# A two-layer diffusion backbone on one core: the first modulation vectors by pieces of columns, sums of squares as products, one tile for two activations

## The chip, the cores and the metric

One core of a Trainium2 chip runs the whole network in one launch. The metric is device time in microseconds (us), the median of several executions. Beside them stands one profiled execution with its own time, from which all durations are taken.

## What is computed

The reference runs two layers over 256 context tokens and 256 latent tokens of width 1024. What matters here is how a layer begins:

```python
m_lat = split(silu(c) @ w_ada[l] + b_ada[l], 9)          # shift, scale, gate for three sub-layers
m_ctx = split(silu(c_ctx) @ w_ada[l] + b_ada[l], 9)
x   = x + 0.5 * gate * swiglu(rmsnorm(x, g) * (1 + scale) + shift)     # FFN, w1 1024 x 5632, w2 2816 x 1024
...                                                                     # mixers, a second FFN
```

So the first FFN of layer 0 needs, before its first product, the root mean square of every token and two of the nine vectors of `w_ada[0]` (shift and scale, 1024 columns each), for both kinds of token.

## The kernel before

Activations are held transposed: `x` is [128 partitions, 8 chunks of features, 512 tokens], context tokens first. Every dense product is float32 in three float32r products: a weight tile [128 x 1024] is loaded as `raw`, cast on ScalarE to `whi` (`split`, L219), and VectorE makes the rest `wlo` (L220); the activations are split the same way into a high and a low half. `three` (L232 to L234) then adds up high x low, high x high and low x high; I call these three products a triple. Each triple that calls `tick()` moves the object `beside` one step on, and generators that were registered with `beside.at(gen, ticks)` run their next part at those ticks: that is how norms, attention stages and loads are put between products. The order on TensorE is the program's own; a scheduler orders the other engines by priority (`tc.high_priority`) and by edges (`tc.issue_after`).

`cold_start` (L413) is the begin of layer 0. `square_sum` (L252) squares a chunk on ScalarE and adds it on VectorE into `ssq`, 16 times; `rstd_cols` and `rstd_rows` (L260, L276) make rows of 1/rms through TensorE. `ada_first` (L158) makes one quarter of shift and scale: 512 columns of `w_ada0` in four DMAs of 512 KB, with packets of 2 KB, each followed by 8 small products of `sc` (the SiLU of c and c_ctx in a 32 wide weight) at L169, then a copy (L174), a transposition (L177) and a few VectorE operations of 4 elements (L182, L184). `norm_part` (L286) makes one chunk of the normed input `h` for one kind of token: `u` on VectorE (L289), the high half on ScalarE (L291), the low half on VectorE (L292). The first halves of scale and shift come before the first triple; the second halves are made by `beside` at the ticks of `COLD`, between the triples of chunks 0 to 3 of the six first weight tiles (two tiles at a time, 24 triples). Then the 24 triples of chunks 4 to 7 follow. All these loads go through one queue, SP's, in the program's order.

Later in the layers, `h` (input of an FFN or of the mixers) and `y` (the merged mixer output) are two tiles with one tag and one buffer, so that the first write of the one waits for the last read of the other. Stages of attention heads run at the ticks listed in `A0`, `A3` and `AT_LAT`.

Of the kernel before, what the change touches and what calls it, by code (L numbers as in the profile page):

```python
# [16 lines left out]
P = 128  # L17
# [23 lines left out]
A0 = (10, 12, 18, 20, 23, 25, 27, 30, 32, 35, 37, 39)  # L41
# [5 lines left out]
              n=(14, 17, 29, 32, 36, 39), n3=(14, 20, 34, 40, 46, 52))  # L47
AT_FULL = dict(d0=A0, d=A1, d3=A2, n=A3, n3=A4)
NORM = (400, 4, 0)
SPREAD = (360, 440, 360, 1)  # L50
EARLY = 2
COLD = ((4, 6, 8, 10, 12, 13), (10, 12, 14, 16, 17, 18))
# [59 lines left out]
def tile_backbone(ctx: ExitStack, tc: tile.TileContext, I, out: bass.AP):  # L112
# [45 lines left out]
    def ada_first(l, mod, part, room):  # L158

        pa = psum()  # L160
        c0 = mod * D + part * 512
        for k2 in range(KC // 2):
            raw = room[:, k2, :]
            nc.sync.dma_start(out=raw.rearrange("p (k c) -> p k c", k=2),
                              in_=I["w_ada0"][k2 * 256:(k2 + 1) * 256, c0:c0 + 512].rearrange("(k p) c -> p k c", k=2))
            for k in range(2):
                kc = 2 * k2 + k
                for j in range(4):
                    mm(pa[32 * j:32 * j + 32, 0:P], sc[:, kc, :], raw[:, k * 512 + j * P:k * 512 + (j + 1) * P],  # L169
                       start=kc == 0, stop=kc == KC - 1)  # L170
            yield
        rows = np_.tile([P, 256], F32, tag="rows", name="rows", bufs=1)[:, 0:P]
        with tc.high_priority(offset=AHEAD):
            nc.scalar.copy(rows, pa[:, 0:P])  # L174
        yield
        pt = psum()
        nc.tensor.transpose(pt[:, 0:P], rows, ident)  # L177
        ks = slice(4 * part, 4 * part + 4)
        v = pt[:, 0:P].rearrange("p (j c) -> p j c", j=4)
        with tc.high_priority(offset=AHEAD):  # L180
            for cls in range(2):
                nc.vector.tensor_tensor(modT[l][:, mod, cls, ks], v[:, :, cls], b_ada[:, l, mod, ks], ALU.add)  # L182
                if mod % 3 == 1:
                    nc.vector.scalar_tensor_tensor(amod[l][:, mod // 3, cls, ks], modT[l][:, mod, cls, ks], 1.0,  # L184
                                                   norm_g[:, l, mod // 3, ks], ALU.add, ALU.mult)
# [30 lines left out]
    def split(hi, lo, src, behind=None):  # L216

        with tc.issue_after(behind) if behind else nullcontext():
            nc.scalar.copy(hi, src)  # L219
        nc.vector.tensor_sub(lo, src, hi.bitcast(F32))  # L220

    def weights(src, n=1024, extra=None, soon=False, room=None, behind=None):
# [3 lines left out]
        with tc.high_priority(offset=AHEAD if soon else WSOON):  # L226
            split(hi[:, :n], lo[:, :n], raw[:, :n], behind)
        return hi, lo
# [21 lines left out]
    ssq = cp.tile([P, T], F32, name="ssq")  # L250

    def square_sum(dt, cs):  # L252
# [4 lines left out]
        nc.scalar.activation(sq, x[:, dt, cs], AF.Square)  # L257
        nc.vector.tensor_tensor(ssq[:, cs], ssq[:, cs], sq, ALU.add)

    def rstd_cols(cs):  # L260
# [6 lines left out]
        with tc.high_priority(offset=AHEAD):  # L267
            nc.vector.tensor_reduce(out=r[:, :n], in_=p1[:, 0:n * P].rearrange("p (t c) -> p t c", t=n),
                                    axis=AX.X, op=ALU.add)
            nc.vector.tensor_scalar(r[:, :n], r[:, :n], 1.0 / D, EPS, ALU.mult, ALU.add)  # L270
            nc.gpsimd.tensor_tensor(r[:, :n], r[:, :n], half[:, :n], ALU.pow)
# [14 lines left out]
    def norm_part(l, which, h, kc, cls, rb):  # L286
# [5 lines left out]
        nc.vector.scalar_tensor_tensor(h[1][:, kc, cs], u, shift, h[0][:, kc, cs].bitcast(F32),  # L292
                                       ALU.add, ALU.subtract)
# [67 lines left out]
    def ada_all(vectors, pool, junk):  # L361
        if not vectors:
            return
        scb = pool.tile([P, 2, 512], F32, name="scb")
# [12 lines left out]
    def ffn(l, i, classes, out_classes_next, before, vectors):  # L377
# [4 lines left out]
        h = split_pair("h") if both else before  # L382
# [30 lines left out]
        def cold_start(n):  # L413

            rooms = glo.before(F32, [P, KC, 1024])
            scale, shift = ([ada_first(l, 3 * which + what, part, rooms[:, 4 * (1 - what):4 * (1 - what) + 4, :])
                             for part in (0, 1)] for what in (1, 0))
            for dt in range(KC):
                for at in SLICES:
                    square_sum(dt, at)  # L420
            rows = [rstd_rows(at) for at in SLICES]
            next(scale[0])
            for r in rows:
                next(r)
            rb = junk.rearrange("p (a t) -> p a t", a=2)
            for cls, r in enumerate(rows):
                next(scale[0])
                nc.scalar.copy(rb[:, cls], next(r)[:, 0:256])
            ws = []

            def load(ks):
                for k in ks:
                    ws.append(w1_unit(k, room=kept(k) if k < 4 else None, soon=k < 2))

            for _ in scale[0]:
                pass
            load(range(EARLY))
            for _ in shift[0]:
                pass
            load(range(EARLY, n))  # L440
            pts = [psum() for _ in range(n)]
            beside.at(scale[1], COLD[0])
            beside.at(shift[1], COLD[1])
            for part, order in enumerate(((0, 2, 4), (4, 0, 2))):
                if part:
                    beside.drain()
                with tc.high_priority(offset=AHEAD):
                    for kc in range(4 * part, 4 * part + 4):
                        for cls in (0, 1):
                            norm_part(l, which, h, kc, cls, rb[:, cls])  # L450
                for k in order:
                    for kc in range(4 * part, 4 * part + 4):
# [4 lines left out]
                    if part:  # L457
                        act(k // 2, pts[k], pts[k + 1])
# [74 lines left out]
        for j in range(FIRST // 2 if cold else 2 if both else 1, NF):  # L533
# [4 lines left out]
            else:  # L538
                ws = [w1_unit(k) for k in (2 * j, 2 * j + 1)]
# [60 lines left out]
    def mixers(l, before):  # L600
# [10 lines left out]
        h = split_pair("h", not full)  # L611
# [566 lines left out]
        for hp2 in range(3):  # L1178
            spread([do(merge, 1, hp2, oT, do(na_qk, hp2 + 1))], na_pair(hp2), 3 * nb, 38, AT["n"])
# [7 lines left out]
        y = split_pair("y", not full)  # L1187
# [15 lines left out]
        def ended(dt, pt):  # L1203
            for cls in (0, 1) if full else (1,):
                residual(l, 1, dt, pt, cls, True)
            if not full:

                with tc.high_priority(offset=AHEAD):
# [176 lines left out]
```

## Time and profile before

| what | value |
|---|---|
| median of 3 executions | 2267.32 us (2265.69 to 2268.48) |
| the profiled execution | 2266.51 us, of which 2264.7 us are the span from the first to the last instruction |
| TensorE (PE) busy | 2234.9 us, 99% of the span |
| VectorE (DVE) busy | 1579.1 us, 70% |
| ScalarE (ACT) busy | 934.4 us, 41% |
| bytes moved | 315.53 MB, 139 GB/s on average |

A slice of the span is read best by its stage: the begin, where nothing is loaded yet, has other limits than the rest, where TensorE has no gap for hundreds of microseconds. PE is the products' own row, PEld the loading of weights beside them, SP the queue of DMAs.

### The profile page before, as it was taken

Reading aid. Unit: us, or ns where it says so; the run is one execution under the profiler, and the core shown is the slowest. Engines: PE = TensorE matmul, PEld = TensorE weight load, DVE = VectorE, ACT = ScalarE, POOL = GpSimd, SP = SyncE. Lnnn points to the kernel's source line nnn. Section 1 sums busy time; section 2 is a strip of 40 time slices with the busy share of each in tenths; the row PEclk is TensorE's granted clock in tenths of the full one; section 3 lists DMA queues with packets and bytes.
Section 4 is the critical chain, followed back from the end, with each engine's and each line's share of the span. In section 5 each row is a group of like instructions: output and inputs, shape, how many; then the busy total and the mean of one; then the engine's idle time right before and its main releaser. Section 6 shows DMA issues by size and latency. Waiting matters only on the chain.

```text
span 2264.7 us, 33530 instructions
## 1 busy us (share of the span) xinstructions
PE 2234.9 (99%) x12799; PEld 1935.7 (85%) x12799; DVE 1579.1 (70%) x3388; ACT 934.4 (41%) x1675; POOL 81.3 (4%) x137
## 2 busy tenths in 40 slices
PE   7999999999999999999999999999999999999998
PEld 4888889888888888888888898888898898899998
DVE  5989843887665664676666579998258885768664
ACT  4323222455654553333222232322234675656443
POOL 0000000001001110000000000000000001200000
PEclk9999999999999999999999999999999999999999
DMA  8556542322223332344544436666333244445564
GB/s 305 184 198 204 192 139 89 112 66 75 75 76 93 91 87 84 99 144 140 159 147 149 141 113 208 208 200 195 101 99 112 67 140 121 135 155 169 188 184 131
DMA packets 94033, 315.53 MB, mean 139 GB/s; under 512 B 12928, under 2 KB 13712, under 8 KB 93872
## 3 DMA queue, kind: packets, MB, share of 16 engines
q1 hardware_dynamic: 89072, 308.07, 42.3%
q0 software_dynamic: 2144, 4.36, 1.4%
q8 instruction: 100, 1.64, 0.3%
q10 hardware_dynamic: 2656, 0.96, 0.2%
q14 instruction: 61, 0.50, 0.1%
HBM read 312.30 MB, written 1.05 MB: 138 GB/s over the span
## 4 chain that ended last, share of the span: by engine, by line
PE 86%; issue 9%; DVE 3%; DMA 1%; ACT 1%; SPq 0%; POOLq 0%; POOL 0%; DVEq 0%; ACTq 0%
PE p L232 25%; PE p L233 24%; PE p L234 24%; PE p L649 2%; PE p L650 2%; PE p L651 2%; PE p L674 1%; PE p L916 1%; PE p L1131 1%; PE p L971 1%; PE p L970 1%; PE p L1041 1%; DMA room<-in_w_ada 1%; PE p L893 1%; DVE wlo L220 1%
## 5 line engine op out<-in xcount | busy, mean ns | idle before, releaser
L219 ACT CAST whi<-raw 128x1024 fp32r<-128x1024 f32 (+1 forms) x430 | 444.7, 1035 | 823.7 <-PE p L233 715.7
L220 DVE TENSOR_TENSOR wlo<-raw,whi 128x1024 fp32r<-128x1024 f32 (+1 forms) x430 | 516.6, 1202 | 268.5 <-ACT whi L219 266.8
L232 PE MATMUL p<-h,whi 128*128 128x512 f32 (+1 forms) x1856 | 695.5, 375 | 0.2 <-DVE h L292 0.2
L234 PE MATMUL p<-h,wlo 128*128 128x512 f32 (+1 forms) x1856 | 681.1, 367 | 0.0
L233 PE MATMUL p<-h,whi 128*128 128x512 f32 (+1 forms) x1856 | 681.1, 367 | 0.0
L232 PEld LDWEIGHTS p<-h,whi 128*128 128x128 f32 x1856 | 348.7, 188 | 58.7 <-issue 2.4
L234 PEld LDWEIGHTS p<-h,wlo 128*128 128x128 f32 x1856 | 348.6, 188 | 58.4
L233 PEld LDWEIGHTS p<-h,whi 128*128 128x128 f32 x1856 | 349.1, 188 | 56.5 <-issue 1.9
L233 PE MATMUL p<-ghi,whi 128*128 128x256 f32 (+1 forms) x836 | 278.0, 333 | 0.0
L234 PE MATMUL p<-ghi,wlo 128*128 128x256 f32 (+1 forms) x836 | 277.8, 332 | 0.0
L197 DVE SCALAR_TENSOR_TENSOR junk<-raw,scb 128x512 f32<-128x512 f32 x256 | 176.2, 688 | 112.7 <-DMA raw<-in_w_adaT 112.2
L232 PE MATMUL p<-glo,whi 128*128 128x256 f32 (+1 forms) x616 | 201.9, 328 | 0.0
L197 DVE SCALAR_TENSOR_TENSOR raw<-raw,scb 128x512 f32<-128x512 f32 x256 | 176.8, 690 | 6.2
L233 PEld LDWEIGHTS p<-ghi,whi 128*128 128x128 f32 x836 | 157.9, 189 | 15.4
L234 PEld LDWEIGHTS p<-ghi,wlo 128*128 128x128 f32 x836 | 157.8, 189 | 15.5
L232 PE MATMUL p<-y,whi 128*128 128x256 f32 (+1 forms) x472 | 136.6, 289 | 0.0
L233 PE MATMUL p<-y,whi 128*128 128x256 f32 (+1 forms) x472 | 136.5, 289 | 0.0
L234 PE MATMUL p<-y,wlo 128*128 128x256 f32 (+1 forms) x472 | 136.2, 289 | 0.0
L232 PEld LDWEIGHTS p<-glo,whi 128*128 128x128 f32 x616 | 116.3, 189 | 10.4
L310 DVE SCALAR_TENSOR_TENSOR x<-p,gmod,x 128x256 f32<-128x256 f32 x80 | 36.5, 480 | 81.8 <-PE p L234 81.7
L232 PEld LDWEIGHTS p<-y,whi 128*128 128x128 f32 x472 | 88.7, 188 | 1.8 <-issue 0.2
L233 PEld LDWEIGHTS p<-y,whi 128*128 128x128 f32 x472 | 88.7, 188 | 1.5
(258 smaller groups left out, 2955.6 us busy)
## 6 DMA issues: line engine op xcount, KB each, us to landing
raw<-in_w SPq DMA_DIRECT2D x208, 512.0 KB, 3.5
raw<-in_w_adaT SPq DMA_DIRECT2D x128, 512.0 KB, 3.7
raw<-in_wf SPq DMA_DIRECT2D x106, 512.0 KB, 3.2
raw<-in_w SPq DMA_DIRECT2D x64, 448.0 KB, 3.5
raw<-in_wv SPq DMA_DIRECT2D x24, 512.0 KB, 3.2
raw<-in_wb SPq DMA_DIRECT2D x24, 512.0 KB, 3.3
room<-in_w_ada SPq DMA_DIRECT2D x16, 512.0 KB, 9.5
raw<-in_wo SPq DMA_DIRECT2D x16, 512.0 KB, 3.2
```

Source lines behind the costliest of these rows:

```text
L197: nc.vector.scalar_tensor_tensor(w if cls else junk, w, 1.0, scb[:, cls, :], ALU.mult, ALU.mult, accum_out=acc[:, kc, i, cls:cls + 1])
L219: nc.scalar.copy(hi, src)
L220: nc.vector.tensor_sub(lo, src, hi.bitcast(F32))
L232: mm(dst, w[0][:, wat], a[1][:, aat[0], aat[1]], start=start, stop=False)
L233: mm(dst, w[0][:, wat], a[0][:, aat[0], aat[1]], start=False, stop=False)
L234: mm(dst, w[1][:, wat], a[0][:, aat[0], aat[1]], start=False, stop=stop)
L310: nc.vector.scalar_tensor_tensor(x[:, dt, cs], pt[:, cs], gmod[l][:, which, cls, dt:dt + 1], x[:, dt, cs], ALU.mult, ALU.add)
L649: mm(pts[t], h[0][:, kc, at], w[1][:, wat], start=kc == 0, stop=False)
L650: mm(pts[t], h[0][:, kc, at], w[0][:, wat], start=False, stop=False)
L651: mm(pts[t], h[1][:, kc, at], w[0][:, wat], start=False, stop=kc == KC - 1)
L674: nc.tensor.transpose(pt[:, k * P:(k + 1) * P], a, ident)
L893: mm(pS[:, rs], k[:, at], q[:, rs], start=True, stop=True)
```

## The change

`ada_first` takes pieces of columns instead of quarters: chunks 0, 1, 2, 3 singly and then 4 to 5 and 6 to 7 (`PIECES`). A piece is two DMAs (shift and scale, `ada_load`) of 128 or 256 columns, so that a contiguous run is 512 or 1024 bytes; its 16 products of 128 or 256 columns accumulate in four groups, and a `tensor_reduce` adds the groups after the transposition. `cold_start` squares a chunk of all 512 tokens at once, by turns on ScalarE and VectorE, and adds up on TensorE with products against a column of ones. `awake(m)` issues m products of ones with ones that nothing reads. The triples of a chunk follow its own piece, in the order that `run` calls give. Elsewhere: `h` and `y` share one tile that is never released (`split_pair`), two casts get double priority (`soon=2`), the last square of the mixers' output is put ahead of other work (`issue_after`), some tick lists move, and one kind of `wlo` waits for a mean.

```diff
-A0 = (10, 12, 18, 20, 23, 25, 27, 30, 32, 35, 37, 39)
+A0 = (10, 12, 18, 20, 23, 25, 27, 30, 32, 37, 38, 39)
-              n=(14, 17, 29, 32, 36, 39), n3=(14, 20, 34, 40, 46, 52))
+              n0=(14, 17, 32, 35, 39, 39), n=(14, 17, 29, 32, 36, 39), n3=(14, 20, 34, 42, 48, 54))
-COLD = ((4, 6, 8, 10, 12, 13), (10, 12, 14, 16, 17, 18))
+PIECES = ((0, 1), (1, 2), (2, 3), (3, 4), (4, 6), (6, 8))
...
+    def ada_load(room, e0, e1):
+        w = (e1 - e0) * P
+        got = []
+        for v in (0, 1):
+            at = (2 * e0 + v * (e1 - e0)) % KC
+            raw = room[:, at:at + e1 - e0, :].rearrange("p s c -> p (s c)").rearrange("p (k c) -> p k c", k=KC)
+            nc.sync.dma_start(out=raw, in_=I["w_ada0"][:, v * D + e0 * P:v * D + e0 * P + w].rearrange(
+                "(k p) c -> p k c", k=KC))
+            got.append(raw)
+        return got
...
+        for v, raw in enumerate(raws):
+            for kc in range(KC):
+                g = 32 * (kc % 4)
+                mm(pa[g:g + 32, v * 256:v * 256 + n * P], sc[:, kc, :], raw[:, kc, :], start=kc < 4, stop=kc >= 4)
...
+            for v in (1, 0):
+                nc.vector.tensor_reduce(
+                    out=red[:, v], in_=pt.rearrange("p (v e g c) -> p v e c g", v=2, e=2, g=4)[:, v, 0:n, 0:2, :],
+                    axis=AX.X, op=ALU.add)
+                nc.vector.tensor_tensor(modT[0][:, v, :, ks], ...)
+                if v:
+                    nc.vector.scalar_tensor_tensor(amod[0][:, 0, :, ks], ...)
...
-    def split_pair(name, half_line=False):
-        both = hp.tile([P, 2 * KC * T + 16], F32R, tag="h", name=name)
+    home = []
+    def split_pair(half_line=False):
+        if not home:
+            home.append(hp.tile([P, 2 * KC * T + 16], F32R, tag="h", name="h"))
+        both = home[0]
...
+            for kc in range(KC):
+                sq = sqs[:, kc % 2, :]
+                if kc % 2:
+                    nc.vector.tensor_tensor(sq, x[:, kc, :], x[:, kc, :], ALU.mult)
+                else:
+                    nc.scalar.activation(sq, x[:, kc, :], AF.Square)
+                for t in range(NT):
+                    mm(p1[:, t:t + 1], sq[:, t * P:(t + 1) * P], ones[:, 0:1], start=kc == 0 and t == 0,
+                       stop=kc == KC - 1, skip_group_check=True)
...
+            load((0, 1))
+            raws.append(ada_load(room, *PIECES[1]))
+            load((2, 3))
+            raws.append(ada_load(room, *PIECES[2]))
+            load(range(4, n))
+            raws.append(ada_load(room, *PIECES[3]))
...
+            begun(0)
+            awake(4)
+            ended(0)
+            with tc.issue_after(lead[1, 0, "lo"]):
+                for f in rests:
+                    f()
+            begun(1)
+            awake(7)
+            run(0, 0)
+            ended(1)
+            run(1, 0)
+            run(0, 2)
+            begun(2)
+            run(1, 2)
+            ended(2)
+            run(2, 0, 2)
+            begun(3)
+            run(0, 4)
+            ended(3)
+            run(1, 4)
+            run(2, 4)
+            run(3, 0, 2)
+            beside.at(piece(4), (1, 2))
+            run(3, 4)
+            beside.drain()
+            beside.at(piece(5), (4, 8))
+            run(4, 0, 2, 4)
+            beside.drain()
+            for k in (0, 2, 4):
+                run(5, k)
+                act(k // 2, pts[k], pts[k + 1])
...
-                ws = [w1_unit(k, soon=k < 2, room=kept(k), behind=lead[0, 3] if k > 1 else None) for k in range(4)]
+                ws = [w1_unit(k, soon=2 if k < 2 else 0, room=kept(k), behind=lead[0, 3] if k > 1 else None)
+                      for k in range(4)]
...
-                ws = [w1_unit(k) for k in (2 * j, 2 * j + 1)]
+                ws = [w1_unit(k, behind=mean[-1] if k % 2 else None) for k in (2 * j, 2 * j + 1)]
...
+                    if dt == KC - 1:
+                        for ins in (squared[-1], summed[-1]):
+                            e.enter_context(tc.issue_after(ins))
```

`begun(i)` issues the products and the copy of piece i, `ended(i)` its transpositions, the VectorE operations behind them and `norm_part` of its chunks; `run(i, k)` issues the triples of piece i's chunks with weight tiles k and k + 1.

TensorE before, at the begin, up to the first triples and the first burst of small products between them (`room` holds the columns of `w_ada0`, `ghi` here the high and low halves of the first weight tiles):

```order
L169 MATMUL p<-room,sc 32x128 x8
L177 MATMUL p<-c_ident,rows 128x128
L169 MATMUL p<-room,sc 32x128 x32
L177 MATMUL p<-c_ident,rows 128x128
L232 MATMUL p<-h,ghi 128x512
L233 MATMUL p<-h,ghi 128x512
L234 MATMUL p<-h,ghi 128x512
...
```

Here 16 small products at a time precede nothing but transpositions, and then the triples follow without a break.

TensorE now, from the transpositions of piece 0 to the triples of piece 1 (L177 are the small products of a piece, L186 its transpositions, L465 `awake`, L250 to L252 the triple):

```order
L186 MATMUL p<-c_ident,sqs 128x128 x2
L177 MATMUL p<-room,sc 32x128 x16
L465 MATMUL p<-ones 128x128 x7
L250 MATMUL p<-h,ghi 128x512
L251 MATMUL p<-h,ghi 128x512
L252 MATMUL p<-h,ghi 128x512
L250 MATMUL p<-h,ghi 128x512
L251 MATMUL p<-h,ghi 128x512
L252 MATMUL p<-h,ghi 128x512
L186 MATMUL p<-c_ident,sqs 128x128 x2
L250 MATMUL p<-h,ghi 128x512
L251 MATMUL p<-h,ghi 128x512
```

The first triple now stands behind the products of piece 1 and seven `awake` products, only two triples stand between them and the transpositions of piece 1, and the triple right behind those transpositions is of piece 1's own chunk.

VectorE now, over the same stretch (L191 to L197 are the small operations behind a transposition, L234 a `wlo` or its like, L313 and L316 are `u` and the low half of `h`):

```order
L234 TENSOR_TENSOR ghi<-raw,ghi 128x1024
L191 TENSOR_REDUCE red<-p 128x2 x2
L194 TENSOR_TENSOR modT_94<-red,c_b_ada 128x2 x2
L234 TENSOR_TENSOR ghi<-raw,ghi 128x1024
L197 SCALAR_TENSOR_TENSOR amod_96<-modT_94,c_norm_g 128x2
L313 SCALAR_TENSOR_TENSOR u<-x,amod_96,junk 128x256 x2
L316 SCALAR_TENSOR_TENSOR h<-u,modT_94,h 128x256 x2
L234 TENSOR_TENSOR wlo<-raw,whi 128x1024 x2
L191 TENSOR_REDUCE red<-p 128x2 x2
```

In piece 1 the low half of a weight tile stands in the middle of the small operations, ahead of `u`; in piece 2 such work stands ahead of them.

The queue of SP before (`raw` are weight tiles, `room` quarters of `w_ada0`):

```order
L136 DMA x<-in_xT 128x512 x8
L164 DMA room<-in_w_ada 128x2x512 x4
L224 DMA raw<-in_w 128x1024 x2
L164 DMA room<-in_w_ada 128x2x512 x4
L224 DMA raw<-in_w 128x1024 x4
L164 DMA room<-in_w_ada 128x2x512 x8
```

Four quarters of `w_ada0` are asked for in the order scale, shift, scale, shift, and two weight tiles after the first.

The queue of SP now:

```order
L135 DMA x<-in_xT 128x512 x8
L164 DMA room<-in_w_ada 128x8x128 x2
L238 DMA raw<-in_w 128x1024 x2
L164 DMA room<-in_w_ada 128x8x128 x2
L238 DMA raw<-in_w 128x1024 x2
L164 DMA room<-in_w_ada 128x8x128 x2
L238 DMA raw<-in_w 128x1024 x2
L164 DMA room<-in_w_ada 128x8x128 x2
L164 DMA room<-in_w_ada 128x8x256 x4
```

Half as many bytes of `w_ada0` now stand ahead of the first triple (1 MB twice instead of 2 MB twice), in shorter runs, and the first weight tiles stand between the pieces.

## Rows read from the trace of the kernel before

**Rows 1.** The page: busy time of each engine (share of the span) and instructions.
```profile
PE 2234.9 (99%) x12799; PEld 1935.7 (85%) x12799; DVE 1579.1 (70%) x3388; ACT 934.4 (41%) x1675; POOL 81.3 (4%) x137
```

**Rows 2.** What TensorE waited for: us in total, times, longest.
```profile
PE p L169 <- DMA room<-in_w_ada: 12.2, 3, 11.9
PE p L232 <- DVE h L292: 3.1, 3, 1.8
PE p L265 <- DVE ssq L258: 2.4, 3, 1.1
PE p L674 <- DVE nsm L1102: 0.8, 1, 0.8
...
PE p L674 <- DVE de L1026: 0.7, 1, 0.7
```

**Rows 3.** Busy time by stretch (PE, PEld, DVE, ACT, POOL), granted clock, DMA share, GB/s.
```profile
10.00:20.00 10.00, 7.30 (x81) 4.34 (x85) 3.84 (x15) 4.03 (x11) 1.39 (x2) 1.00 1.04 408
20.00:30.00 10.00, 7.35 (x74) 4.40 (x63) 8.04 (x18) 5.96 (x12) 0.00 (x0) 0.89 1.02 395
...
27.70:31.20 3.50, 3.50 (x10) 2.35 (x8) 3.50 (x8) 3.50 (x6) 0.00 (x0) 0.51 1.00 358
```

**Rows 4.** Timeline to the first triple: start, us, what, idle before and releaser.
```profile
23.23 1.08 PE L169 MATMUL p<-room,sc 128*32 128x128 f32 x16 [0.17 <-DMA room<-in_w_ada]
...
24.44 0.27 ACT L174 COPY rows<-p 128x128 f32<-128x128 f32 x1 [3.43 <-PE p L169]
...
24.76 0.33 PE L177 MATMUL p<-c_ident,rows 128*128 128x128 f32 x1 [0.44 <-ACT rows L174]
25.12 0.23 DVE L182 TENSOR_TENSOR modT<-p,c_b_ada 128x4 f32<-128x4 f32 x2 [1.42 <-PE p L177]
25.32 1.31 ACT L291 ACTIVATE h<-u,modT 128x256 fp32r<-128x256 f32 x3 [0.61 <-DVE modT L182]
...
26.89 0.47 PE L232 MATMUL p<-h,ghi 128*128 128x512 f32 x1 [1.80 <-DVE h L292]
```

**Rows 5.** TensorE's timeline: a burst of small products between triples.
```profile
37.62 0.39 PE L234 MATMUL p<-h,ghi 128*128 128x512 f32 x1
37.94 1.08 PE L169 MATMUL p<-room,sc 128*32 128x128 f32 x32
38.95 0.50 PE L232 MATMUL p<-h,ghi 128*128 128x512 f32 x1
```

**Rows 6.** TensorE's timeline: begin of cold_start's last 16 triples, product behind them.
```profile
56.75 0.39 PE L232 MATMUL p<-h,ghi 128*128 128x512 f32 x1
...
67.63 0.39 PE L232 MATMUL p<-h,whi 128*128 128x512 f32 x1
```

**Rows 7.** DMA queue: packets, MB, share of 16 engines; 10:14, 404.9:405.9, 406.5:407.9 us.
```profile
q1 hardware_dynamic: 835, 1.61, 104.7%
...
q10 hardware_dynamic: 245, 0.22, 69.1%
...
q10 hardware_dynamic: 144, 0.03, 10.6%
```

**Rows 8.** Groups by line and form on VectorE, first 60 us: busy, mean ns.
```profile
L289 DVE SCALAR_TENSOR_TENSOR u<-x,amod,junk 128x256 f32<-128x256 f32 x16 | 6.9, 480 | 0.0
...
L220 DVE TENSOR_TENSOR ghi<-raw,ghi 128x1024 fp32r<-128x1024 f32 x4 | 4.8, 1219 | 0.0
...
L182 DVE TENSOR_TENSOR modT<-p,c_b_ada 128x4 f32<-128x4 f32 x8 | 0.9, 157 | 13.9 <-PE p L177 13.9
```

**Rows 9.** Timeline, six float32 products of 130 columns and the next product.
```profile
467.65 0.83 PE L916 MATMUL p<-v,w 128*128 128x130 f32 x6
468.23 0.48 PE L232 MATMUL p<-h,whi 128*128 128x512 f32 x1
```

**Rows 10.** Timeline: the norm in front of layer 0's second FFN.
```profile
958.99 1.31 ACT L291 ACTIVATE h<-u,modT 128x256 fp32r<-128x256 f32 x3 [1.42 <-PE p L234]
...
960.11 0.39 PE L232 MATMUL p<-h,ghi 128*128 128x256 f32 x1 [1.16 <-DVE h L292]
```

More of the change, by code (lines that the diff above doesn't have):

```diff
@@ L381, in ffn @@
         both = len(classes) == 2
-        h = split_pair("h") if both else before
+        h = split_pair() if both else before
         w1 = I["w1"][l, i]
@@ L413, in cold_start @@
         def cold_start(n):
[L415 to L428, printed above, removed]
+            room = glo.before(F32, [P, KC, 1024])
+            raws = [ada_load(room, *PIECES[0])]
+            sqs = pool.tile([P, 2, 512], F32, tag="scb", name="sqs", bufs=1)
+            p1 = psum()
+            for kc in range(KC):
+                sq = sqs[:, kc % 2, :]
+                if kc % 2:
+                    nc.vector.tensor_tensor(sq, x[:, kc, :], x[:, kc, :], ALU.mult)
+                else:
+                    nc.scalar.activation(sq, x[:, kc, :], AF.Square)
+                for t in range(NT):
+                    mm(p1[:, t:t + 1], sq[:, t * P:(t + 1) * P], ones[:, 0:1], start=kc == 0 and t == 0,
+                       stop=kc == KC - 1, skip_group_check=True)
@@ L429, in cold_start, with awake @@
+            r = np_.tile([P, 4], F32, tag="r", name="r")
+            with tc.high_priority(offset=AHEAD):
+                nc.vector.tensor_scalar(r, p1[:, 0:NT], 1.0 / D, EPS, ALU.mult, ALU.add)
+                nc.gpsimd.tensor_tensor(r, r, half[:, 0:NT], ALU.pow)
             ws = []
+            pts = [psum() for _ in range(n)]
+            def awake(m):
+                for _ in range(m):
+                    mm(pts[n - 1][:, 0:P], ones, ones, start=True, stop=True)
             def load(ks):
@@ L432, in load @@
                 for k in ks:
[L433 to L446, printed above, removed]
+                    ws.append(w1_unit(k, room=kept(k) if k < 4 else None, soon=k < 1, rest=rests if k == 1 else None))
@@ L447, in cold_start, with ended, run @@
+            def ended(i):
+                next(going[i], None)
                 with tc.high_priority(offset=AHEAD):
-                    for kc in range(4 * part, 4 * part + 4):
+                    for kc in range(*PIECES[i]):
                         for cls in (0, 1):
                             norm_part(l, which, h, kc, cls, rb[:, cls])
-                for k in order:
-                    for kc in range(4 * part, 4 * part + 4):
+            def run(i, *ks):
+                for k in ks:
+                    for kc in range(*PIECES[i]):
@@ L456, in cold_start, with piece @@
                             tick()
-                    if part:
-                        act(k // 2, pts[k], pts[k + 1])
+            def piece(i):
+                begun(i)
+                yield
+                ended(i)
+                yield
+            awake(6)
+            p2 = psum()
+            for t in range(NT):
+                nc.tensor.transpose(p2[:, t * P:(t + 1) * P], r[:, t:t + 1].to_broadcast([P, P]), ident)
+            with tc.high_priority(offset=AHEAD):
+                nc.scalar.copy(junk, p2)
+            begun(0)
[29 more added lines that the diff above has]
+                act(k // 2, pts[k], pts[k + 1])
         def warm_start():
@@ L1186, in mixers @@
         tgs.append(gate(2, 7, "t2k"))
[L1187 removed]
+        y = split_pair(not full)
         for d2 in range(4):
```

78 lines of the change are left out of this document (41 added, 37 removed).

## The prediction

> **What bounds the kernel now.** I read the page first: TensorE is busy for 2234.9 of 2264.7 us [rows 1], so only some 30 us can be gained by better order; everything else would need fewer products, and the change removes none of the large ones. The table of waits then tells where these 30 us are: 12.2 us are waits of the first small products for columns of `w_ada0`, 1.8 of the 3.1 us for `h` stand at the first triple, and what is left is five or six single gaps of 0.7 to 1.2 us far behind [rows 2]. So the begin is a stage of its own. In it the DMA engines are full (408 and 395 GB/s from 10 to 30 us [rows 3]), the last burst of small products that the first triple needs waits for its columns until 23.23, and the first triple starts at 26.89 [rows 4]. From there on TensorE never stops again in the begin: the last of the 48 triples of `cold_start` is followed by the next weight tile's at 67.63 [rows 6]. The begin is therefore bounded by transport up to 23, by a chain of small operations up to 26.89, and by TensorE after that. What follows 67.63 is TensorE without gaps, so a begin that ends later by a microsecond makes the kernel later by a microsecond.
>
> The 40.74 us from 26.89 to 67.63 come apart like this. The last 16 triples take 10.88 us, 0.68 each [rows 6]; 48 of them take 32.6. A burst of 32 records of small products costs 38.95 - 37.62, less the 0.23 of the triple's own product, and 0.1 for the slower restart: 1.2 [rows 5]; the 128 records that lie between the triples, in seven bursts, come to 5.8. Between 27.7 and 31.2 the granted clock was 0.51, the level of 1.2 GHz, after TensorE had idled most of 24.4 to 26.9 [rows 3, 4]; at half speed 3.4 us lose some 1.6. Together 40.0; the rest is transpositions and seams.
>
> **The start.** Ahead of the first triple the queue now carries x (2.10 MB), piece 0, two weight tiles and piece 1 (1.05 MB each): 5.24 MB instead of 7.34. 2.10 MB less at 400 GB/s [rows 3] are 5.2 us. Against that stand runs of 512 bytes. A 2 KB packet takes 85 ns: 104.7% of 16 engines for 4 us are 67 us, for 786 packets (1.61 MB); a 1 KB packet takes 50 ns (69.1% of 16 us, 215 packets), one of 256 bytes some 17 ns (10.6% of 22.4 us, 144 packets) [rows 7]. Between the last two I read 28 ns for 512 bytes. A piece has 2048 packets, 128 per engine: 3.6 us, where 2 KB packets would need 2.7; two pieces lose 1.8. Bounds: a quarter of the 2 KB packet (21 ns, nothing lost) and the price of the 1 KB packet (50 ns, 3.7 us lost per piece). I take 28 because both neighbours are measured. So piece 1 lands at 23.2 - 5.2 + 1.8 = 19.8 (18.0 to 25.4). The Trainium skill, "DMA: Bandwidth & Descriptors", section "Why small descriptors are slow (HBM only)", counts 3 cycles per packet beside one per 32 bytes; by that 512 bytes cost only 1.13 times what they cost within 2 KB, an estimate, and the sum below would be 1.1 us less. No run here has shown such packets on SP's queue.
>
> After the landing half of piece 1's records are left (1.08 at the slow clock [rows 4], 0.9 with the next one's overlap), then seven `awake` products, 14 records. Six records of 130 columns took 0.58 us [rows 9], so these take 1.4 to 1.5, and 3.0 at the lower clock. First triple: 19.8 + 0.9 + 1.5 = 22.2, that is 4.7 earlier. Piece 0's own chain does not set it: it lands 6.2 before piece 1 (a piece at 3.6 and two weight tiles at 2.6), and its four `awake` products, chain and one 1.22 weight rest [rows 8] end near 21. The 32 products with a column of ones replace 14 additions on VectorE; x is first in the queue, and each chunk's products run while the next chunk and then piece 0 arrive, so I cost them at nothing. Without that cover their 64 records would cost 6 us at 0.1 each [rows 9].
>
> **The waits that come in.** Each piece has a chain from its transposition to its first triple. Before, the transposition at 24.76 led to VectorE at 25.12, the first `h` at 25.32 and the triple at 26.89, with `u` already made [rows 4]: 0.36 to VectorE, and 1.57 from `h` to the triple. Now come five small operations (157 ns each, overlapping [rows 8]; I take 0.5) and one `u` (0.43 in a row; 480 ns alone [rows 8]) between: 0.36 + 0.5 + 0.43 + 1.57 = 2.9. The order shows what TensorE has beside it. For piece 1 nothing: the triple behind the transpositions needs that very chunk, and VectorE also has a weight rest of 1.22 [rows 8] in the middle: 4.1. Piece 2, again nothing: 2.9. Piece 3 has four triples (2.7) in between: hidden. Piece 4 has two chunks, four transpositions and four `u`, and nothing beside it: 3.8. Piece 5 has four triples: 0.5 is left. Sum 11.3 us, bounded below by 8 (no weight rest in the way, each chain half a microsecond shorter).
>
> The small products of pieces 2 to 5 among the triples: two bursts at 1.2 and two of twice the columns at 2.1 [rows 5], 6.6 against 5.8. Transpositions of pieces 3 and 5: 0.7. The clock: before, an idle stretch of 2.2 us in all brought one spell at 1.2 GHz; now there are three waits of 2.9 to 4.1 and the products before the first triple. I count one spell, 1.6; none or three are the bounds. The begin then ends at 22.2 + 32.6 + 6.6 + 0.7 + 11.3 + 1.6 = 75.0, against 67.63: **7.4 us later**.
>
> **The rest.** The gaps aimed at are 0.7 (L674 for `de`), 0.8 (for `nsm`), 1.1 at L265 and 1.2 at the norm of layer 0's second FFN, where the first `h` waits for the last product of `y` [rows 2, 10], with two or three smaller ones; all together 5.8 at most. The moved ticks should end most of the L674 gaps, as a tick or more of products then stands in front. At the norm I take nothing: with `h` free earlier, VectorE still has two weight rests (2.4) and the last residual in line before the sums, and the gap comes a few products later. The last square moved forward saves one VectorE operation. I take 2.4 (from -0.5, a weight rest in the wrong place, to 5.8).
>
> **Sum.** 2266.5 (the profiled execution) + 7.4 - 2.4 = 2271.5. It ran 0.8 under the median shown, so 2272.3 on the scale of the medians: slower by 5.0, 0.22%. I count as no change what lies within 0.2%, 4.5 us: about what a measurement of this kernel can tell.
>
> **Rivals.** (1) Not slower, because the start is earlier than I make it: 512-byte packets pass at the rate of 2 KB ones (1.8 less) and `awake` keeps the clock at 2.4 GHz through the waits (1.6 less). Place: the products of piece 1 and the waits behind them; it decides when piece 1 lands before 18.5 and no granted clock under 1 shows after the first triple. Then 2272.3 - 3.4 = 2268.9; with most of the small gaps closed (3 more) 2266. For it: 400 GB/s at 2 KB, a full queue; against it: 1 KB packets already cost 50 ns, not 42 [rows 7]. (2) Faster: TensorE does not wait for the chains, because weight rests and loads keep the triples back anyway or the chains are far shorter. Without 11.3 and 1.6 the begin ends at 62.1, 5.5 earlier, and the kernel takes 2259.4. For it: in the row of before, 2.1 us passed from transposition to triple, not 2.9; against it: the order has no product beside three of the five chains. (3) Slower still: a 512-byte packet costs what a 1 KB one does; piece 1 lands 5.6 later and the kernel takes 2277.9. For it: only that the neighbours are few packets on another queue. (4) The change does not do what it says, `awake` leaves the clock low at the first triple: 1.5 for seven products, then 1.6 for each spell, 2275.
>
> **How the numbers follow.** My forecast 0.33, rival 3 and 4 together 0.15: slower 0.48. Rival 1, no change: 0.38. Rival 2, faster: 0.14. The low end takes rival 1 with all small gaps closed, 2263.5; the high end rival 3 with one more spell, 2280; rival 2 is left out. The forecast's own range is 2269 to 2277.
>
> **What would show it.** Right: in the new trace the first triple at 21 to 24; TensorE waits for L316 of 2.5 to 4.5 us right behind the transpositions of pieces 1, 2 and 4; the next weight tile's product near 75. Wrong: waits for `h` under 8 us in all, a first triple before 20, the last of the 48 triples ended before 70, or gaps saved behind 500 us of more than 4.

## The result, and the profile after

The changed kernel takes 2285.84 us (median of four executions), the kernel before 2267.70 us beside it: ratio 1.0082, 95% interval [1.0068, 1.0096]. Three of the four lie at 2284.20 to 2285.94 us; the fourth took 5811.0 us, is left out of the ratio, and stays unexplained. It is **slower by some 18 us**, where I forecast 5; the time lies above my range. The profiled execution ran 2285.94 us with a span of 2284.2, 19.5 more than before.

The page first. TensorE is still 99% busy, but with 19.0 us more of busy time [rows 1] for 42 more instructions: so in sum it does something slowly and waits no more than before. The next table shows that this sum hides an exchange of waits.

```profile
PE 2253.9 (99%) x12841; PEld 1955.5 (86%) x12841; DVE 1579.6 (69%) x3393; ACT 932.1 (41%) x1664; POOL 82.0 (4%) x136
```

What TensorE waited for (us in total, times, longest): the 12.2 us for columns of `w_ada0` [rows 2] are gone, and 11.7 us for the low half of `h` (L316) stand in their place. The first product waits for the first square of x (5.5 us).

```profile
PE p L250 <- DVE h L316: 11.7, 8, 3.9
PE p L452 <- ACT sqs L450: 5.5, 1, 5.5
PE p L289 <- DVE ssq L282: 2.3, 4, 1.6
```

The timeline of TensorE to the first triple (start, us, what, idle before and its releaser):

```profile
5.52 13.79 PE L452 MATMUL p<-ones,sqs 128*128 128x1 f32 x64 [5.52 <-ACT sqs L450]
19.16 2.91 PE L465 MATMUL p<-ones 128*128 128x128 f32 x12
21.86 1.06 PE L513 MATMUL p<-c_ident,r 128*128 128x128 f32 x4
22.86 1.94 PE L177 MATMUL p<-room,sc 128*32 128x128 f32 x32
24.72 1.36 PE L465 MATMUL p<-ones 128*128 128x128 f32 x8
25.92 0.38 PE L186 MATMUL p<-c_ident,sqs 128*128 128x128 f32 x2
26.23 1.08 PE L177 MATMUL p<-room,sc 128*32 128x128 f32 x32
27.25 1.83 PE L465 MATMUL p<-ones 128*128 128x128 f32 x14
30.53 0.50 PE L250 MATMUL p<-h,ghi 128*128 128x512 f32 x1 [1.46 <-DVE h L316]
```

The 64 records of the products with a column of ones (L452) fill TensorE from 5.52 to 19.30 us without a gap, 0.215 us each. The whole chain to the first triple stands behind them in the engine's order: the transpositions of 1/rms (L513), the small products of pieces 0 and 1 (L177), `awake`. The first triple is at 30.53, 3.6 us later than before [rows 4].

That TensorE, not the squares, is late shows on the other two engines: each square waits for its buffer, which TensorE still reads (timeline of ScalarE and VectorE in the same stretch).

```profile
7.45 0.63 ACT L450 ACTIVATE sqs<-x 128x512 f32<-128x512 f32 x1 [2.08 <-PE p L452]
9.10 0.69 DVE L448 TENSOR_TENSOR sqs<-x 128x512 f32<-128x512 f32 x1 [2.43 <-PE p L452]
```

Behind the first triple come the waits for `h`, and the last row is the product behind the 48 triples of `cold_start`, at 67.63 before [rows 6]:

```profile
32.05 0.38 PE L186 MATMUL p<-c_ident,sqs 128*128 128x128 f32 x2
...
33.01 1.23 DVE L234 TENSOR_TENSOR ghi<-raw,ghi 128x1024 fp32r<-128x1024 f32 x1
...
36.35 0.79 PE L250 MATMUL p<-h,ghi 128*128 128x512 f32 x1 [3.92 <-DVE h L316]
...
47.49 0.50 PE L250 MATMUL p<-h,ghi 128*128 128x512 f32 x1 [2.63 <-DVE h L316]
...
65.72 0.50 PE L250 MATMUL p<-h,ghi 128*128 128x512 f32 x1 [2.77 <-DVE h L316]
...
80.19 0.50 PE L250 MATMUL p<-h,ghi 128*128 128x512 f32 x1 [0.18 <-DVE h L316]
...
87.12 0.39 PE L250 MATMUL p<-h,whi 128*128 128x512 f32 x1
```

Pieces 1, 2, 4 and 5 wait 3.92, 2.63, 2.77 and 0.18 us, together 9.5. The weight rest of 1.23 us at 33.01 stands in the middle of piece 1's chain. The begin ends 19.5 us later, which is the whole difference of the spans; all that follows it is worth nothing in sum.

Busy time by stretch shows the granted clock (the column behind POOL) after the two longest idle stretches:

```profile
35.40:42.20 6.80, 5.85 (x22) 4.20 (x25) 3.25 (x4) 2.26 (x3) 0.00 (x0) 0.50 1.08 360
66.10:69.60 3.50, 3.50 (x10) 2.73 (x9) 0.85 (x2) 0.51 (x1) 0.00 (x0) 0.51 0.00 0
```

Two spells at 1.2 GHz, 10.2 us in all, in place of one of 3.4 [rows 3]. TensorE idled for 0.95 of the first and worked for 5.85 (first number behind the length), so it worked for 9.3 us at half speed: they cost 4.6 us.

### The profile page after: what moved, and what is told of

Read it like the earlier page. It is cut to its first block, busy times and chain, and to the rows that moved or that the text cites. A ratio compares the mean times of both kernels' runs of the same rounds, so it can differ in the third digit from the quotient of the medians.

```text
span 2284.2 us, 33599 instructions
## 1 busy us (share of the span) xinstructions
PE 2253.9 (99%) x12841; PEld 1955.5 (86%) x12841; DVE 1579.6 (69%) x3393; ACT 932.1 (41%) x1664; POOL 82.0 (4%) x136
## 4 chain that ended last, share of the span: by engine, by line
PE 87%; issue 9%; DVE 3%; ACT 1%; DMA 0%; POOL 0%; POOLq 0%; DVEq 0%; SPq 0%; ACTq 0%
PE p L250 24%; PE p L251 24%; PE p L252 24%; PE p L739 2%; PE p L740 2%; PE p L741 2%; PE p L764 1%; PE p L1006 1%; PE p L1221 1%; PE p L1061 1%; PE p L1060 1%; PE p L1131 1%; PE p L983 1%; PE p L452 1%; DVE wlo L234 0%
## 5 line engine op out<-in xcount | busy, mean ns | idle before, releaser
L250 PE MATMUL p<-h,whi 128*128 128x512 f32 (+1 forms) x2328 | 832.2, 357 | 0.2 <-DVE h L316 0.2
L251 PE MATMUL p<-h,whi 128*128 128x512 f32 (+1 forms) x2328 | 817.7, 351 | 0.0
L252 PE MATMUL p<-h,wlo 128*128 128x512 f32 (+1 forms) x2328 | 817.4, 351 | 0.0
L234 DVE TENSOR_TENSOR wlo<-raw,whi 128x1024 fp32r<-128x1024 f32 (+1 forms) x430 | 516.6, 1202 | 278.6 <-ACT whi L233 277.1
L250 PEld LDWEIGHTS p<-h,whi 128*128 128x128 f32 x2328 | 437.5, 188 | 60.7 <-issue 3.0
L252 PEld LDWEIGHTS p<-h,wlo 128*128 128x128 f32 x2328 | 437.0, 188 | 59.8
L251 PEld LDWEIGHTS p<-h,whi 128*128 128x128 f32 x2328 | 437.9, 188 | 58.0 <-issue 1.9
L252 PE MATMUL p<-ghi,wlo 128*128 128x256 f32 (+1 forms) x836 | 277.7, 332 | 0.0
L250 PE MATMUL p<-glo,whi 128*128 128x256 f32 (+1 forms) x616 | 201.9, 328 | 0.0
L252 PEld LDWEIGHTS p<-ghi,wlo 128*128 128x128 f32 x836 | 157.8, 189 | 15.5
L250 PEld LDWEIGHTS p<-glo,whi 128*128 128x128 f32 x616 | 116.3, 189 | 10.3
L739 PE MATMUL p<-wlo,h 128*128 128x512 f32 x192 | 76.5, 398 | 0.0
L740 PE MATMUL p<-whi,h 128*128 128x512 f32 x192 | 75.3, 392 | 0.0
L741 PE MATMUL p<-whi,h 128*128 128x512 f32 x192 | 75.3, 392 | 0.0
L233 ACT CAST ghi<-g 128x512 fp32r<-128x512 f32 (+1 forms) x88 | 49.7, 565 | 48.3 <-DVE g L424 48.2
L250 PE MATMUL p<-olo,whi 128*128 128x512 f32 (+1 forms) x192 | 67.2, 350 | 0.0
```

The lines of the kernel that those rows point to most:

```text
L250: mm(dst, w[0][:, wat], a[1][:, aat[0], aat[1]], start=start, stop=False)
L251: mm(dst, w[0][:, wat], a[0][:, aat[0], aat[1]], start=False, stop=False)
L252: mm(dst, w[1][:, wat], a[0][:, aat[0], aat[1]], start=False, stop=stop)
L739: mm(pts[t], h[0][:, kc, at], w[1][:, wat], start=kc == 0, stop=False)
L740: mm(pts[t], h[0][:, kc, at], w[0][:, wat], start=False, stop=False)
L741: mm(pts[t], h[1][:, kc, at], w[0][:, wat], start=False, stop=kc == KC - 1)
```

## The experiments

The end of the begin is the start of the product behind the 48 triples, from each run's trace.

| run | first triple | end of the begin | time, us | ratio to before, 95% interval |
|---|---|---|---|---|
| before | 26.89 | 67.63 | 2267.70 | 1 |
| the change | 30.53 | 87.12 | 2285.84 | 1.0082 [1.0068, 1.0096] |
| 1 sums put back | 21.79 | 78.88 | 2278.46 | 1.0049 [1.0036, 1.0063] |
| 2 the rest alone | 26.94 | 67.68 | 2267.47 | 1.0003 [0.9994, 1.0011] |
| 3 nine products of ones ahead | 31.67 | 88.56 | 2286.08 | 1.0079 [1.0064, 1.0095] |
| 4 chains one step earlier | 29.06 | 71.19 | 2271.17 | 1.0018 [1.0009, 1.0028] |
| 5 both edits, 1 and 4 | 22.70 | 65.76 | 2264.24 | 0.9990 [0.9982, 0.9999] |
| 6 sums as products in the kernel before | 30.97 | 72.94 | 2270.93 | 1.0018 [1.0009, 1.0027] |
| 7 eighteen products of ones ahead | 28.74 | 84.76 | 2284.93 | 1.0083 [1.0069, 1.0097] |
| 8 both edits, 1 KB packets | 26.73 | 69.65 | 2268.51 | 1.0009 [1.0000, 1.0018] |
| 9 both edits, piece 0 ahead of 1/rms | 21.66 | 64.63 | 2265.47 | 0.9992 [0.9983, 1.0001] |

The kernel before stood beside each batch at 2266.7 to 2267.0.

### 1. The sums put back

```diff
-            for kc in range(KC):
-                sq = sqs[:, kc % 2, :]
...
-                for t in range(NT):
-                    mm(p1[:, t:t + 1], sq[:, t * P:(t + 1) * P], ones[:, 0:1], start=kc == 0 and t == 0,
-                       stop=kc == KC - 1, skip_group_check=True)
+            for dt in range(KC):
+                for at in SLICES:
+                    square_sum(dt, at)
+            for t in range(NT):
+                nc.tensor.transpose(p1[:, t * P:(t + 1) * P], ssq[:, t * P:(t + 1) * P], ident)
```

> The changed kernel with the sums of squares made as before (squares on ScalarE, sums on VectorE, 256 columns at a time) and everything else as changed. Theory A: the 64 records of products with a column of ones, 0.21 us each at the lower clock, set the start; then the first triple moves from 30.5 to 22 to 24 us and the kernel to 2277 to 2279 us. Theory B: the 512-byte packets of pieces 0 and 1 set the start and the sums only fill the wait; then the first triple stays at 29 to 31 and the kernel at 2285 to 2287.

Measured 2278.46, 7.4 us under the change. In the timeline of TensorE the first triple now follows `awake` without a wait:

```profile
19.02 1.08 PE L177 MATMUL p<-room,sc 128*32 128x128 f32 x32
...
21.48 0.39 PE L462 MATMUL p<-ones 128*128 128x128 f32 x2
21.79 0.50 PE L250 MATMUL p<-h,ghi 128*128 128x512 f32 x1
...
27.61 0.79 PE L250 MATMUL p<-h,ghi 128*128 128x512 f32 x1 [3.93 <-DVE h L316]
```

The sums are worth 8.7 us at the first triple. 21.79 lies near my 22.2, but the path isn't the one forecast: the products of piece 1 start at 19.02 and wait for no columns, so TensorE's own chain sets the start here and not the transfer, for which I had 19.8. The wait at piece 1 is untouched, 3.93 us. And run 1 is still 11.5 us slower than the kernel before (2266.96 beside it) where I forecast 5, so the sums aren't the whole miss.

### 2. The rest of the change alone

The kernel before keeps its `ada_first` and `cold_start`; all else (one tile for `h` and `y`, casts, tick lists, the moved square) is as changed.

> The begin of before, all the rest as changed (one tile for h and y, casts ahead, ticks, square ahead). The forecast's term: 2.4 us gained, about 2265 us. Rival, from the trace of the changed kernel, where the gaps behind 500 us add up to 5.4 instead of 6.9 us: 1 us gained or less, 2266 to 2268. If the rest cost time, over 2269.

Measured 2267.47, no difference, in the rival's band. The waits of TensorE, and one stretch (granted clock behind POOL):

```profile
PE p L236 <- DVE h L302: 2.4, 3, 1.8
PE p L275 <- DVE ssq L268: 2.0, 3, 1.6
PE p L685 <- DVE nsm L1113: 1.0, 1, 1.0
```

```profile
962.60:966.00 3.40, 3.27 (x17) 3.30 (x18) 2.95 (x8) 1.25 (x3) 0.86 (x1) 0.54 0.06 24
```

The gap of 0.7 for `de` [rows 2] is gone, and the waits for `h` are 0.7 less in sum. But the longest wait for `ssq` grew from 1.1 to 1.6 and the one for `nsm` from 0.8 to 1.0, and TensorE was busy for 2236.6 us, 1.7 more than before [rows 1]. Behind the wait of 1.6 us for `ssq`, at the norm of layer 0's second FFN, this execution has a spell at half speed of 3.4 us, which accounts for these 1.7 us; the kernel before waits there in two parts (1.16 [rows 10] and 1.1 us) and has none. That isn't the whole reason: the changed kernel has the same wait of 1.6 us without a spell (granted clock 1.00 from 980 to 990, products of 256 columns at 0.28 us), and there too all that follows the begin is worth nothing. Some gaps closed by moving; why the time did not follow stays open.

### 3 and 7. Products of ones ahead of the sums

```diff
+            for _ in range(9):
+                mm(pts[n - 1][:, 0:P], ones, ones, start=True, stop=True)
             for kc in range(KC):
                 sq = sqs[:, kc % 2, :]
```

Run 7 has 18 in place of 9.

> The changed kernel with nine more products of ones with ones ahead of the sums of squares, in time in which TensorE was idle. Theory A1: the sums are slow because of the clock; if TensorE is at 2.4 GHz when x lands, a record takes 0.11 instead of 0.21 us, the sums end 5 to 7 us earlier and the kernel takes 2279 to 2281 us. A2: the clock stays low in spite of them, or a record takes 0.21 us at either clock; then 2286 to 2288 us.

> The changed kernel with 18 products of ones by ones ahead of the sums (9 of them changed nothing). Theory C (a record of a one-column product costs 0.21 us because TensorE runs at its lower level there): by the end of the 18 the records go from 0.213 to 0.112 us, as they do after 16.4 in the run with the sums put back, the 64 records then take 7 to 8 us in place of 13.7, and although the sums start at 11 they end by 19; time 2282 to 2285. Theory D (0.21 us is what such a record takes at either level, its load of 128 columns of weights setting it): the sums take 13.7 us again and end at 25; time 2289 to 2291.

With nine (18 records) the sums took 13.65 us again, and began 1.8 us later (timeline). The time, 2286.08, is in the band of A2.

```profile
3.33 4.21 PE L447 MATMUL p<-ones 128*128 128x128 f32 x18 [3.33 <-POOL half L143]
7.33 13.65 PE L455 MATMUL p<-ones,sqs 128*128 128x1 f32 x64
```

Alone, this run would have said that 0.21 us is simply what such a record takes. With eighteen the sums took 9.05 us, and busy time by stretch shows how (PE's records in brackets, granted clock behind POOL):

```profile
3.40:8.10 4.70, 4.70 (x22) 4.70 (x23) 0.95 (x3) 0.63 (x1) 0.16 (x1) 1.00 0.93 314
8.20:9.70 1.50, 1.50 (x15) 1.50 (x15) 0.00 (x0) 0.00 (x0) 0.00 (x0) 1.00 1.03 367
9.80:15.00 5.20, 5.20 (x48) 5.20 (x48) 1.38 (x2) 1.83 (x3) 0.00 (x0) 1.00 1.10 381
15.05:18.60 3.55, 3.55 (x18) 3.55 (x19) 0.69 (x1) 0.01 (x1) 0.00 (x0) 0.50 1.13 358
```

22 records of products of ones in 4.70 us are 0.21 each; from 8.2 they take 0.10 to 0.11. The one-column records begin at that price (48 in 5.2 us, 0.11 each), and from 15.05 on they take 0.20 again, with a granted clock of 0.50. So the price of a record follows the clock for both kinds, and in this run the clock fell while TensorE had no gap and ran nothing but one-column products. At the upper level throughout, 64 records would take some 7 us (64 x 0.11, an estimate), which still stand ahead of everything. In time, run 7 lies where the theory of the clock put it (2282 to 2285), but at 2284.93 it isn't to be told from the change itself: its four times lie from 2283.75 to 2288.28. In its trace the begin ends 2.4 us sooner; whether products that keep TensorE awake bring more here than they cost is not shown.

### 4. The chains one step earlier

```diff
             awake(7)
-            run(0, 0)
             ended(1)
-            run(1, 0)
-            run(0, 2)
+            run(0, 0)
             begun(2)
-            run(1, 2)
+            run(0, 2)
             ended(2)
-            run(2, 0, 2)
+            run(1, 0, 2)
             begun(3)
...
```

Pieces 4 and 5 are begun and ended in the same manner between triples, no longer at ticks.

> The changed kernel with the same work in another order on TensorE: the transpositions of a piece come two to eight triples before the first triple that needs them. Theory A: the waits of 3.9, 2.6 and 2.8 us for h and the two spells at the lower clock behind them come from the order; they go, and the kernel takes 2271 to 2276 us. Rival C: what the triples wait for is late anyway (weight rests, columns); the waits come back elsewhere and the kernel stays over 2281 us.

Measured 2271.17, 14.7 us under the change. Waits from 15 to 100 us, the stretch from 20 to 100 us, and the products of piece 0:

```profile
PE p L186 <- ACT sqs L179: 1.2, 1, 1.2
PE p L252 <- DVE ghi L234: 0.6, 1, 0.6
```

```profile
20.00:100.00 80.00, 78.09 (x515) 62.16 (x515) 61.35 (x155) 31.95 (x51) 0.46 (x1) 1.00 0.65 214
```

```profile
22.45 1.08 PE L177 MATMUL p<-room,sc 128*32 128x128 f32 x32
```

No wait for `h` is left, the granted clock of the stretch is 1.00, and no product of 512 columns in it takes the 0.63 us of the lower level. From the first triple to the end of the begin the traces differ by 14.5 us (56.6 against 42.1). Of these 9.5 are the waits between the triples and 4.6 the two spells: 14.1. The first triple comes 1.5 us sooner as well (29.06). That isn't the edit, for up to the `awake` behind piece 1's products the order on TensorE is that of the change: the products of piece 0 run at the upper level here (1.08 us) and took 1.94 in the change. The same difference is part of the 8.7 us of run 1.

### 5. Both edits

> The changed kernel with both edits: the sums of squares back on ScalarE and VectorE, and the pieces' small products, transpositions and h asked for one step earlier in TensorE's order. Theory: the two costs are apart from one another and add, 7.4 us (the first edit alone) and 14.7 us (the second alone), so 2285.8 - 22.1 = 2263.7, forecast 2262 to 2266, first triple near 21.8 and the last of the first 48 before 67, no wait for h over 1 us. Rival: with the first triple 7 us sooner, pieces 2 to 4 arrive too late for their place, TensorE waits for the transfer instead of for h, and the gain stops at 2268 or above.

Measured 2264.24; the two costs add in the times, as forecast (2263.7).

```profile
22.70 0.47 PE L250 MATMUL p<-h,ghi 128*128 128x512 f32 x1
...
25.97 0.64 PE L177 MATMUL p<-room,sc 128*32 128x128 f32 x16 [1.06 <-DMA room<-in_w_ada]
...
65.76 0.39 PE L250 MATMUL p<-h,whi 128*128 128x512 f32 x1
```

```profile
PE p L177 <- DMA room<-in_w_ada: 1.7, 2, 1.1
```

The begin ends 1.9 us before that of the kernel before, and TensorE's only waits from 15 to 100 us are 1.7 us for columns of `w_ada0`. In the traces the sum is not full: the begin ends 8.2 and 15.9 us sooner with one edit and 21.4 with both, 2.8 less than together. These new waits, of the kind that the rival named, and the 1.5 us of run 4's start can account for that. The ratio, 0.9990 [0.9982, 0.9999], lies just below one, but by less than the 0.2% that I call a change: it is as fast as the kernel before, and hardly faster.

### 6. The sums as products in the kernel before

The edit of run 1 the other way round: in the kernel before, `square_sum` is replaced by the 32 products with a column of ones.

> The kernel before with one part of the change alone: the sums of squares as 32 products with a column of ones on TensorE. Theory (the price of the sums is what stands in TensorE's order behind them): the 64 records take 13.8 us again, from 5.5 to 19.3, the products of w_ada that began at 11.9 start at 19, their data has long landed, and the first triple comes 4 to 6 us after its 26.9; time 2271 to 2274. Rival 1 (my forecast: nothing, the transfer of w_ada covers them): 2267 to 2269. Rival 2 (the full price of the changed kernel, whose first chain is shorter): 2275 or above.

Measured 2270.93, 4.2 us over the 2266.74 beside it, just under the 2271 to 2274 of the theory.

```profile
5.26 13.78 PE L427 MATMUL p<-ones,sqs 128*128 128x1 f32 x64 [5.26 <-ACT sqs L425]
18.98 1.93 PE L169 MATMUL p<-room,sc 128*32 128x128 f32 x32
...
30.97 0.50 PE L232 MATMUL p<-h,ghi 128*128 128x512 f32 x1 [1.71 <-DVE h L292]
...
72.94 0.39 PE L232 MATMUL p<-h,whi 128*128 128x512 f32 x1
```

The same 13.78 us. The first small products of `w_ada0` now start at 18.98 instead of 11.9 [rows 2]; but half of what the first triple needs arrives later than that anyway [rows 4], so 4.1 us of the delay reach it and not all. The price of the sums is what of the first chain stands behind them while its data has already landed.

### 8 and 9. What bounds the begin once both are mended

Run 8 is run 5 with `PIECES = ((0, 2), (2, 4), (4, 6), (6, 8))`, so packets of 1 KB. Run 9 is run 5 with the first piece's products put ahead of 1/rms:

```diff
-            awake(6)
+            begun(0)
+            awake(2)
             p2 = psum()
...
-            begun(0)
             awake(4)
```

> The run with both edits, but w_ada in four pieces of two column blocks in place of six, so that all packets of it have 1 KB and none 512 B. Theory (a transfer of 512-byte packets moves as many bytes per us as one of larger ones, 350 to 410 GB/s in the rows of both kernels): nothing is gained from the packets, the first piece of twice the bytes lands 2 to 3 us later, and so does the first triple; 2 to 4 us slower than both edits, 2265 to 2268. Rival (512-byte packets cost nearly as much as 1 KB ones): the first piece lands as early as before and all later ones earlier, and the time is that of both edits or up to 3 us less.

> The run with both edits, in which the first piece's small products stand ahead of the four transpositions that carry 1/rms, in the time in which TensorE ran products of ones (4 products of ones less). The data of that piece landed at 14.3 us in that run and its products began at 17.55. Theory (the transfer of w_ada and w1 bounds the begin by now): the first triple comes 1.5 to 2.5 us sooner than 22.7, but piece 3 lands at 26 as before, TensorE waits for it by as much longer, and the time stays within 1 us of both edits, 2263.5 to 2265.5. Rival (the chain to the first triple still sets the begin): 2262.5 or less.

Run 8: 2268.51, 4.3 us over run 5, the first triple 4.0 later; a little more than expected. DMA queue from 10 to 12 us, run 8 and then run 5 (packets, MB, share of 16 engines), and what TensorE waited for in run 8:

```profile
q1 hardware_dynamic: 752, 0.77, 108.4%
```

```profile
q1 hardware_dynamic: 1308, 0.69, 113.2%
```

```profile
PE p L177 <- DMA room<-in_w_ada: 5.5, 4, 1.8
```

The larger packets did carry more, 0.77 MB against 0.69 in the same 2 us, so the theory's equal rate is off by a tenth. But the first two pieces are twice as large, and TensorE waits 5.5 us for columns where it waited 1.7. Run 8 changes the size of packets and of pieces together; larger packets with pieces of the old size were not tried.

Run 9: 2265.47, at the upper edge of the band expected, and not to be told from run 5 (their intervals overlap). The first triple came 1.0 us sooner, not 1.5 to 2.5, because the second piece is now waited for as well:

```profile
19.28 0.65 PE L177 MATMUL p<-room,sc 128*32 128x128 f32 x16 [0.79 <-DMA room<-in_w_ada]
...
25.76 0.64 PE L177 MATMUL p<-room,sc 128*32 128x128 f32 x16 [1.70 <-DMA room<-in_w_ada]
```

The third piece is waited for until 25.76 where it was 25.97, with 1.70 us in front instead of 1.06. The transfer bounds the begin here, though the begin still ended 1.1 us sooner in the trace; that the time did not follow is within the scatter of the runs (2263.21 to 2268.14), and stays open.

## Why the prediction was wrong

The direction and the places of the waits were right, the size was not, and the start went the other way (forecast 4.7 us sooner, measured 3.6 later). The direction isn't luck, for run 1, without the price of the sums, is slower too. In numbers: 2271.5 on the scale of the profiled execution against 2285.94, a miss of 14.4 us. By its own terms:

| term | forecast | measured |
|---|---|---|
| 512-byte packet | 28 ns | 27 ns |
| first triple | 22.2 | 30.53, missed by 8.3 |
| waits for `h`, pieces 1 / 2 / 4 / 5 | 4.1 / 2.9 / 3.8 / 0.5 | 3.92 / 2.63 / 2.77 / 0.18 |
| the clock, behind the first triple | 1.6 (one spell) | 4.6 (half of the 9.3 worked in two spells) |
| triples, small products, transpositions, seams | 39.9 | 42.5, what is left; not taken apart |
| end of the begin | 75.0 | 87.12, missed by 12.1 |
| the rest | -2.4 | 0, missed by 2.4 |

**The step that failed** is the one that reads "The 32 products with a column of ones replace 14 additions on VectorE; ... so I cost them at nothing." It held three errors. The price: I named 6 us at 0.1 each, from products in the middle of the kernel [rows 9], where TensorE runs at its upper level; here, as the first thing TensorE does, a record took 0.215. The cover: I took the arrival of x and piece 0 as cover, but at 0.215 the products of a chunk (8 records, 1.7 us) take longer than the chunk's transfer, and the last chunk's end at 19.30. And the place: nothing in the first chain may pass them in TensorE's order, and the transpositions of 1/rms, both pieces' products and the `awake` groups come after, 9.8 us from 19.30 to the end of the last group. I had bounded this term by nothing and by 6 us and then left the upper bound out of the range. Run 6 shows the same price in the other kernel. Run 1 puts the remainder of the start within 0.4 us of the forecast, but that is in part luck: I had set TensorE's chain through piece 0 aside as done near 21, and it is this chain that sets the start there. It ends beside the transfer (products of piece 1 at 19.02, its columns at 19.28 in run 9).

**The clock** was the second step: "I count one spell, 1.6; none or three are the bounds". Two came. The second lasted 3.4 us and cost 1.7, as priced; the first, behind 3.92 us of idle with little work before it, lasted 6.8 us, twice the one of the kernel before [rows 3], and cost 2.9. Of rival 4 the condition fell, for the level was up before the first triple (the last 14 records of `awake` took 1.83 us, not 3.0); its "1.6 for each spell" had the mechanism behind the first triple, with the size of the first spell too small.

**The rest** was forecast from the gaps that the moved operations aimed at; run 2 gives 1.0003 [0.9994, 1.0011]. I had written for the norm that "the gap comes a few products later". Run 2 agrees for `ssq` and `nsm`, whose longest waits grew; for the other gaps it isn't shown.

**What held.** The waits for `h`: read from the order alone and priced by the chain before, 11.3 against 9.5, with the weight rest in the middle of piece 1's chain. Rival 2, no waits, fell: run 4 shows that these waits with their clock cost 14.1 us in the traces, 14.7 in the time, most of the loss of 18. With the 7.4 us of the sums that is more than the loss, because without both the change is a little faster than the kernel before (run 5). Rival 3 fell too: the DMA queue of the changed kernel, from 10.2 to 11.8 us, where nearly all packets have 512 bytes (packets, MB, share of 16 engines), gives

```profile
q1 hardware_dynamic: 1094, 0.56, 114.7%
```

114.7% of 16 engines for 1.6 us are 29.4 us, 27 ns a packet. (At 1 KB run 8's queue took 46 ns, 108.4% of 16 engines for 2 us, where I had read 50.) The estimate from the page of the Trainium skill that the prediction cited ("DMA: Bandwidth & Descriptors", section "Why small descriptors are slow (HBM only)") was 1.13 times a quarter of the 85 ns of a 2 KB packet, 24 ns: nearer than the next neighbour (50 ns at 1 KB), a little too low, and the measurement decides. The transfer was right: in run 9, which asks for it in the same order, the second piece is there at 19.28, against the 19.8 forecast. It wasn't what the first triple waited for in the change.

Beyond the forecast, the change's own idea is sound: with the additions left where they were and each chain asked for one step earlier (run 5), the begin ends 1.9 us sooner than before. Its two faults, 22 us by runs 1 and 4, outweigh that tenfold. Not tried: each `awake` group taken out by itself.

## What to carry to other kernels

An operation that is free on an idle engine is free only if nothing on the path stands behind it in that engine's order; price it at the level the engine runs at in that place, not at the level it has in the steady state. Where a chain over three engines lies between two products, ask for it at least one chain's length of other products earlier: a wait of 3 to 4 us was paid here and then paid half again by the clock. And a bound that was written down belongs in the range.

## What was not expected of the hardware

A float32 product of one column cost as much as one of 128 columns: 0.21 us a record at the lower level and 0.11 at the upper, both with a weight of 128 columns loaded for each (runs 3 and 7, and the change). Three rows put this beside each other: 64 records at 128x1 in 13.79 us, 12 at 128x128 in 2.91 (0.24 each, with the end of the last), and in run 7 48 records at 128x1 in 5.2.

The granted clock fell to 0.50 in run 7 at 15.05 us, after 5.2 us of one-column products without a gap; a busy TensorE is thus no proof of a high clock. And at the start the profile's clock says less than the records do: it reads 1.00 from 5.5 to 19.2 in the change and from 3.4 to 8.1 in run 7, where the records take the 0.21 us that they take at 0.50 from 15.05 to 18.6. In run 2 it reads 1.00 even behind the first triple, where products of 512 columns take 0.63 us to 30.0 and 0.39 from 30.5 on:

```profile
27.70:31.20 3.50, 3.50 (x12) 2.68 (x10) 3.50 (x8) 3.50 (x6) 0.00 (x0) 1.00 0.98 341
```

```profile
29.63 0.63 PE L236 MATMUL p<-h,ghi 128*128 128x512 f32 x1
```

Early in a trace the duration of a known product is the better clock.
